# A two-layer transformer kernel: how the position bias rows are repeated 128 times through device memory

## Chip, cores and metric

The kernel runs on one core of a Trainium2 chip, as one program. The metric is the device time of one execution in microseconds (us). The kernel before takes 2340.94 us, the median of 3 runs (2340.61 to 2341.34).

## What is computed

The reference is one block of a first model (four mixers side by side, then a gated feed-forward layer) and two layers of a second model (an attention layer, then a retention layer), on 256 tokens of width 2048 in float32. The change touches the first mixer, an attention with three branches whose scores all get a position bias from a small table:

```python
def rel_bias_heads(dist, table):
    b = table[rel_bucket(dist)].astype(jnp.float32)
    b = jnp.moveaxis(b, -1, 0)
    return b.reshape(NSA_KV_HEADS, NSA_GQA, *dist.shape)
...
    s_w = jnp.einsum('btgrd,bsgd->bgrts', qblk, kw).astype(jnp.float32) * scale + rel_bias_heads(d_w, rel_table)
    p_w = masked_softmax(s_w, m_w)
```

The bias of a head depends only on the distance between query and key. So one row of 512 numbers per head (eight heads) holds all of it, and the score tile of 128 queries needs that row once per query, shifted by one element from each query to the next.

## The kernel before

**The weight stream.** All the weights pass through the core once, in units of at most 128 x 1024 float32 (512 KB). `load` (line 354) issues a unit's load on the SP queue into one of four tiles `wf`; `prefetch` (362) lets ACT round it to its high part `wh` (line 374), and `low` lets DVE make the low part `wl` (line 387), in four tiles each. A `wf` tile is free for the next load when its `wl` is made. PE multiplies with both parts: `job_N` (455) has the tokens stationary and makes three products per step (lines 473, 474, 475), `job_T` (416) has the weights stationary and makes two (lines 449, 450). The jobs run in the order of `plan`.

**The jobs around the change.** After the queries (512 columns) comes the job of the keys `kn` (line 692, 280 columns), then that of the values `vn` (line 693, 256 columns, 16 k tiles x 2 token tiles x 3 products = 96 products, in four units of 512 KB), then the first projection of the fourth mixer, `ev_dqk(0)` (line 923, 16 k tiles x 2 column tiles = 32 pairs of products), then `ev_dqk(1)` (line 929), between whose products those of line 927 stand. The text calls the four units of the value job V0 to V3 and the first of the next job D0.

**The side programs.** `Sched` (274) steps small programs between the products: each `yield n` lets n ticks of 650 ns of planned PE time go by before the next piece is put into the engines' instruction streams. Every engine executes its stream in order. Three side programs matter here:

- `bias_task` (631) makes the bias rows. PE picks the table's rows with a one-hot matrix, DVE copies the 8 x 512 result to SBUF (`rb`, line 641), and POOL issues four DMAs (line 644), each of which writes two of the eight rows 128 times into a tile `dr` in device memory. POOL then issues four loads (line 652) that read `dr` with a shift of one element per partition into the tiles `bias`.
- `zb_task` (680) gives POOL a few operations (`zT`, `zb`) that fall between the first of those DMAs and the other three.
- `task_qk` (877) normalises queries and keys. POOL squares them (`sqq` and `sqk`, lines 882 and 884), DVE reduces them and scales `qn`, and PE transposes the result (`mA`, lines 902 and 908). It begins after the value job, and its first transposes stand in PE's stream after 23 of the 32 pairs of the next job.

Nothing reads `bias` before `task_A` (line 779), long after these jobs. But POOL's stream has the four loads of line 652 ahead of `sqq`, and each of them waits until the DMA of line 644 that wrote its rows has landed.

Of the kernel before, what the change touches and what calls it, by code (L numbers as in the profile page):

```python
# [18 lines left out]
P = 128  # L19
T = 256  # L20
# [14 lines left out]

# ---------------------------------------------------------------- weight plan
def plan():
# [94 lines left out]
def units(jobs):  # L132
    """(stage, offset, words per partition) of every unit, in the order of use"""
    off, out = {}, []
    for j in jobs:
        st = j["stage"]
        nc_ = sum(len(t[1]) for t in j["tiles"])
        K = len(j["rows"])
        sizes = [(min(j["kc"], K - c) * nc_, False) for c in range(0, K, j["kc"])]
        if j.get("raw"):  # L140
            sizes = [z for n in sizes for z in (n, (1024, True))]
        j["u0"] = len(out)
        for n, raw in sizes:
            assert n <= 1024
            o = off.get(st, 0)
            out.append((st, o, n, raw))
            off[st] = o + P * n
    return out, off


# ---------------------------------------------------------------- constants of the shapes
def shape_consts():
# [52 lines left out]
def pack_inputs(inp):  # L205
    """arrays for the device: layout only"""
    f = {k: np.asarray(v) for k, v in inp.items()}
# [64 lines left out]

# ---------------------------------------------------------------- the program
class Sched:
    """side programs, stepped between the matrix products of the weight stream; a program yields the
    number of ticks to wait, or another program whose end it waits for"""

# [45 lines left out]
class XS:  # L323
    """operand tiles [P, hi | lo]; a side program that still has to write one is run on first use"""

# [9 lines left out]
def body(tc, a, out, stop=None, dbg=None):  # L335
# [13 lines left out]

    # ---- weight stream  # L350
    wf, wh, wl = {}, {}, {}
# [10 lines left out]
    def prefetch(to, alt=None):  # L362
        """high parts of the units before to, low parts of those before to - LAG; all in tiles of alt, if given"""
        to = min(len(us), to)
        while pos["sp"] < to:
            load(pos["sp"] + WFB)
            q = pos["sp"]
            st, o, n, raw = us[q]
            if not raw:
                if alt is None:  # L370
                    wh[q] = pw.tile([P, 1024], F32R, name="wh", tag="wh", bufs=4)
                else:
                    wh[q] = alt.tile([P, 1024], F32R, name="wh", tag="wh", bufs=2)
                ACT.activation(wh[q][:, :n], wf[q][:, :n], AF.Copy)  # L374
            pos["sp"] += 1
        low(to if alt else to - LAG, alt)
# [39 lines left out]
    def job_T(j, xs, evac, tail=1, alt=None, raw=None, one=False):  # L416
        """weights stationary: psum [column, (token by x hi) | (token by x lo)] per 128 columns;
        the last units (tail) go column by column; raw: products with the raw units, between the others;
        one: all three products into the same columns"""
        K, nt, kc = len(j["rows"]), len(j["tiles"]), j["kc"]  # L420
# [34 lines left out]
    def job_N(j, xs, evac):  # L455
        """x stationary: psum [token, column] per 128 tokens"""
        K, kc = len(j["rows"]), j["kc"]
# [25 lines left out]

    # ---- small helpers
    def small(w=1, dt=F32):
        return psm.tile([P, w], dt, name="sm", tag=f"sm{w}", bufs=10 if w <= 2 else 4)

    def rsqrt(dst, src, mul, add, w, np_=P):
        """dst = (src * mul + add) ** -0.5; mul None: src ** -0.5"""
        t = small(w)[:np_]  # L490
# [14 lines left out]
    def split(x, src, g=None):  # L505
        """generator: x[:, :T] = hi, x[:, T:] = lo of src * g"""
        if g is None:
# [8 lines left out]
    def put(xs, n, k, src, g=None):  # L516
        """side program: xs[k] = split of src * g"""
        def gen():
# [9 lines left out]
    def col_sums(pp, tag, tiles):  # L528
        """psum [tok, 2n]: column sums of the n tiles [P, T]"""
        pcs = pp.tile([P, 512], F32, name="pcs", tag=tag)  # L530
# [7 lines left out]
    def rms_rows(pp, tag, ss, n, rc, dg, dst):  # L538
        """generator: rc [tok, 2] = rstd columns of the sums ss [P, T]; dst [P, T] = their row broadcast"""
        ps = col_sums(pp, tag, [ss])  # L540
# [8 lines left out]

    # ---- constants  # L550
    NVEC = 7 * 16 + 2 + 12 + 8 + 16
# [15 lines left out]

    # ================================================================ phase 1: mixers
    p12, p1 = ExitStack(), ExitStack()
# [8 lines left out]
    def load_x(order):  # L578
        """x as 8 tiles of two k tiles each"""
        r = []  # L580
# [50 lines left out]
    def bias_task():  # L631
# [9 lines left out]
        V.tensor_copy(rb[:8, :], pb[:8, :])  # L641
        dr = pd.tile([8, P, 512], F32, name="dr")
        for z in range(4):
            G.dma_start(dr[2 * z:2 * z + 2], rb[2 * z:2 * z + 2, None, :].to_broadcast([2, P, 512]))
            yield 7
        d = dr[:]
        for z in range(4):
            yield 2
            bias[z] = s2("bias", (P, 2, T))
            src = bass.AP(tensor=d.tensor, offset=d.offset + 127 + z * 2 * P * 512,  # L650
                          ap=[[511, P], [P * 512, 2], [1, T]])
            G.dma_start(bias[z], src)
# [16 lines left out]

    # ---- A projections  # L670
    zT = s2("zT", (P, 2, T))
# [23 lines left out]
    def gelu2(x, w, mk, e=G):  # L695
        """generator: 2 * gelu(x) (tanh form)"""
        q = mk("gq")[:, :w]
# [11 lines left out]
    def finish_nat(po, kb, tt, mt):  # L709
        """generator: group rms norm of po [tok, 512] and transposition into xB[kb:kb+4]"""  # L710
        jk = s2("jk")
# [32 lines left out]
    def task_A():  # L744
        # compressed keys and values
        hh = yield from gelu2(hx[:, :30], 30, lambda n: small(32), V)
# [32 lines left out]
        yield tBias  # L779
        # attention batches: heads of one kv group per psum bank  # L780
        for tt in range(2):
# [95 lines left out]
    def task_qk():  # L877
        """queries, keys: rms norm per head, transposition; gates"""
        V.tensor_scalar(gq8, gqk[:, 0:1], 0.125, None, OP.mult)
# [33 lines left out]

    # ---- D projections, with the compression products of A behind the first
    dqk = [[s2("dqk", (P, 2, T)) for _ in range(2)] for _ in range(2)]
# [21 lines left out]

    # ---- D: stick breaking
    def task_D():
# [74 lines left out]

    # ---- C: spatial gating
    cv, cu = [None] * 2, [None] * 2
# [35 lines left out]

    # ---- B: gated short convolution
    braw = [s2("braw", (P, 2, T)) for _ in range(2)]
# [70 lines left out]

    # ---- output projection of the mixers
    acc2 = q1.tile([P, T], F32, name="acc2")
# [57 lines left out]

    # ================================================================ phase 2: feed forward
    t1 = s1
# [66 lines left out]

    # layer norm after a residual sum, on shifted values
    class LN:
        tag = "m"

        def __init__(self, pool, x, pair):
            """x: the operand tiles of the residual; pair(k): the tile of the sums k and k + 1"""  # L1260
            self.base = pool
# [9 lines left out]
        def pre(self):  # L1271
            """side program: xr[k] = ALPHA * x[k]"""
            for k in range(16):
# [25 lines left out]
        def add(self, k):  # L1299
            """xr[k] is complete"""  # L1300
            if k < 8:
# [34 lines left out]
        def sums(self, s, q, last):  # L1336
            """column sums"""
            for z, t in ((0, s), (2, q)):
# [4 lines left out]
        def finish(self):  # L1343
            """row broadcasts [P, T]: rstd in psum and in sbuf, -mean * rstd in psum"""
            ps = self.ps
# [32 lines left out]

    # ================================================================ phase 3: attention
    p3l, p3 = ExitStack(), ExitStack()  # L1380
# [39 lines left out]
    def qk_task(key, which, hi, lo, rs, fold):  # L1420
        """rms norm, rope, transposition of 4 heads; rs [P, head, tt]"""
        x = [raw.pop((key, tt)) for tt in range(2)]
# [37 lines left out]
    def og_task(h, o):  # L1460
        """generator: gate and split; o is in psum or sbuf"""
        s = sl.pop(h)
# [114 lines left out]
    def pair0(k):  # L1577
        """in the operand tiles that are read by then"""
        if k in (0, 14):
# [13 lines left out]
    def decay():  # L1593
        """lgd = log1p(-2 ** -e)"""
        ne, fr, u, t, z = [small(16) for _ in range(5)]
# [71 lines left out]

    # ================================================================ phase 4: retention
    qkr, vhl, onT = {}, {}, {}
    spare = [0]  # L1670

    def xa_tile(name, shape=(P, 512)):
        """scratch in the operand tiles that are free until the gates of the first heads"""
        spare[0] += 1
# [212 lines left out]
```

## Time and profile before

| | us |
|---|---|
| median of 3 runs | 2340.94 |
| lowest and highest run | 2340.61, 2341.34 |
| the profiled execution, first to last instruction (span) | 2356.2 |
| PE busy in it | 2285.8 (97%) |
| DVE busy | 1531.2 (65%) |
| ACT busy | 1141.5 (48%) |
| POOL busy | 418.2 (18%) |

Of the profiled execution only the span is known; it is 15.3 us longer than the median of the runs. PE is the engine to look at: it is busy nearly all the time, so the questions are where its few idle stretches lie and what ends them. "DMA share" in the profile is the busy share of the core's 16 DMA engines. The profile counts POOL's queue of DMAs as q0 (software_dynamic) and the queue of the weight loads, which SP issues, as q1 (hardware_dynamic).

### The profile page before, as it was taken

The numbers are of one execution on the slowest core, as the hardware profiler recorded it, in microseconds if no ns is written. First come the engines' busy times: TensorE is split into PE (matmuls) and PEld (weight loads), VectorE is DVE, ScalarE is ACT, GpSimd is POOL, SyncE is SP. The second block draws the span as 40 slices with busy tenths as digits, with TensorE's granted clock in tenths as the row PEclk, the third lists the DMA queues.
The fourth block names the chain that finished last, engine by engine and source line by source line (L and its number), as shares of the span: only waits on it lengthen the run. The fifth ranks groups of instructions, "written<-read, shape, count | busy, mean of one in ns | idle before, by whom it ended". The sixth has DMA issues, their size and how long they took to land.

```text
span 2356.2 us, 33516 instructions
## 1 busy us (share of the span) xinstructions
PE 2285.8 (97%) x12755; PEld 1969.4 (84%) x12755; DVE 1531.2 (65%) x2372; ACT 1141.5 (48%) x1690; POOL 418.2 (18%) x408
## 2 busy tenths in 40 slices
PE   8599999999999999999999999989999999999997
PEld 7487788888888888888888888878888888888887
DVE  6266688765555555555558898867776766777464
ACT  5246654554443344444444556455444544446343
POOL 3114342111110011110002211461000000001061
PEclk9799999999999999999999999989999999999998
DMA  6554346555656555556565444535555555556543
GB/s 217 139 175 142 99 145 212 186 181 188 189 187 188 187 182 190 183 180 193 180 208 181 149 152 153 171 126 194 173 175 179 179 161 180 171 177 192 185 166 119
DMA packets 118641, 408.56 MB, mean 173 GB/s; under 512 B 16490, under 2 KB 18794, under 8 KB 118480
## 3 DMA queue, kind: packets, MB, share of 16 engines
q1 hardware_dynamic: 113184, 400.80, 52.9%
q0 software_dynamic: 5152, 5.54, 1.4%
q8 instruction: 100, 1.64, 0.3%
q14 instruction: 61, 0.50, 0.1%
q10 hardware_dynamic: 144, 0.08, 0.0%
HBM read 402.15 MB, written 4.19 MB: 172 GB/s over the span
## 4 chain that ended last, share of the span: by engine, by line
PE 81%; DVE 6%; POOL 3%; issue 2%; ACT 1%; POOLq 0%; ACTq 0%; DVEq 0%
PE st L449 40%; PE st L450 21%; PE st L473 5%; PE st L474 4%; PE st L475 4%; DVE wl L387 2%; POOL xr L1294 1%; PE mO L1806 1%; PE st L446 1%; PE st L447 1%; PE mA L851 0%; PE mS L1779 0%; POOL lnq L1321 0%; PE mO L832 0%; PE mT L1824 0%
## 5 line engine op out<-in xcount | busy, mean ns | idle before, releaser
L387 DVE TENSOR_TENSOR wl<-wf,wh 128x1024 fp32r<-128x1024 f32 (+1 forms) x750 | 947.9, 1273 | 336.6 <-ACT wh L374 333.0
L374 ACT ACTIVATE wh<-wf 128x1024 fp32r<-128x1024 f32 (+1 forms) x750 | 788.4, 1055 | 730.9 <-PE st L449 439.9
L449 PE MATMUL st<-xA,wh 128*128 128x512 f32 x2144 | 772.1, 403 | 14.9 <-DVE xA L514 7.0
L450 PE MATMUL st<-xA,wl 128*128 128x256 f32 x2272 | 642.3, 283 | 4.2 <-DVE wl L387 4.2
L449 PE MATMUL st<-xB,wh 128*128 128x512 f32 x1536 | 546.3, 399 | 5.8 <-DVE evs L660 2.8
L449 PEld LDWEIGHTS st<-xA,wh 128*128 128x128 f32 x2144 | 406.4, 190 | 115.7 <-ACT wh L374 7.3
L450 PEld LDWEIGHTS st<-xA,wl 128*128 128x128 f32 x2272 | 433.9, 191 | 6.1 <-DVE wl L387 5.9
L450 PE MATMUL st<-xB,wl 128*128 128x256 f32 x1536 | 430.6, 280 | 0.0
L449 PEld LDWEIGHTS st<-xB,wh 128*128 128x128 f32 x1536 | 289.0, 188 | 76.7 <-DVE xB L1652 4.1
L450 PEld LDWEIGHTS st<-xB,wl 128*128 128x128 f32 x1536 | 290.5, 189 | 1.1
L449 PE MATMUL st<-act,wh 128*128 128x512 f32 x704 | 248.8, 399 | 0.0
L450 PE MATMUL st<-act,wl 128*128 128x256 f32 x704 | 197.7, 281 | 0.0
L474 PE MATMUL st<-wl,xB 128*128 128x512 f32 x448 | 174.8, 390 | 0.8 <-DVE wl L387 0.8
L473 PE MATMUL st<-wh,xB 128*128 128x512 f32 x448 | 175.4, 391 | 0.0
L475 PE MATMUL st<-wh,xB 128*128 128x512 f32 x448 | 174.5, 390 | 0.0
L449 PEld LDWEIGHTS st<-act,wh 128*128 128x128 f32 x704 | 132.3, 188 | 33.0
L660 DVE TENSOR_TENSOR evs<-st,evt 128x256 f32<-128x256 f32 x110 | 46.1, 422 | 151.2 <-ACT evt L658 151.2
L450 PEld LDWEIGHTS st<-act,wl 128*128 128x128 f32 x704 | 133.0, 189 | 0.0
L1207 POOL TENSOR_TENSOR evs<-evs,R 128x256 f32<-128x256 f32 x44 | 32.4, 735 | 487.3 <-DVE evs L660 487.3
L1750 POOL TENSOR_TENSOR rm<-qkr,c 128x512 f32<-128x512 f32 x16 | 32.5, 2031 | 456.3 <-DVE qkr L1684 451.7
L474 PEld LDWEIGHTS st<-wl,xB 128*128 128x128 f32 x448 | 84.2, 188 | 17.7 <-DVE wl L387 1.6
L475 PEld LDWEIGHTS st<-wh,xB 128*128 128x128 f32 x448 | 84.1, 188 | 17.7
(425 smaller groups left out, 2621.4 us busy)
## 6 DMA issues: line engine op xcount, KB each, us to landing
wf<-in_w_c SPq DMA_DIRECT2D x264, 512.0 KB, 4.2
wf<-in_w_e SPq DMA_DIRECT2D x256, 512.0 KB, 4.0
wf<-in_w_d SPq DMA_DIRECT2D x112, 512.0 KB, 3.6
wf<-in_w_a SPq DMA_DIRECT2D x84, 512.0 KB, 3.7
wf<-in_w_b SPq DMA_DIRECT2D x32, 512.0 KB, 4.3
xr<-in_xT SPq DMA_DIRECT2D x16, 256.0 KB, 5.9
wf<-in_w_a SPq DMA_DIRECT2D x5, 420.0 KB, 3.9
dr<-rb POOLq DMA_DIRECT2D x4, 512.0 KB, 48.2
```

Of the source, the lines that this page charges most:

```text
L374: ACT.activation(wh[q][:, :n], wf[q][:, :n], AF.Copy)
L387: V.tensor_tensor(wl[q][:, :n], wf[q][:, :n], wh[q][:, :n].bitcast(F32), OP.subtract)
L446: PE.matmul(ps[m][:, :T], hv[:, cs], x[:, :T], start=kk == 0, stop=False)
L447: PE.matmul(ps[m][:, :T], hv[:, cs], x[:, T:], start=False, stop=False)
L449: PE.matmul(ps[m], hv[:, cs], x, start=kk == 0, stop=False)
L450: PE.matmul(ps[m][:, :T], lv[:, cs], x[:, :T], start=False, stop=kk == K - 1)
L473: PE.matmul(p, xh, h[:, o:o + n], start=kk == 0, stop=False)
L474: PE.matmul(p, xh, l[:, o:o + n], start=False, stop=False)
L475: PE.matmul(p, xl, h[:, o:o + n], start=False, stop=kk == K - 1)
L660: V.tensor_tensor(s, p[:, :T], t, OP.add)
L1207: G.tensor_tensor(s, s, R2, OP.mult)
L1750: G.tensor_tensor(m, x[:, ::-1], rsn.rearrange("p (a t) -> p a t", a=2), OP.mult)
```

## The change

The eight rows are first written once, by one DMA, to a tile `d0` of 8 x 512 in device memory (16 KB). A second DMA then reads those 16 KB 128 times (a step of 0 in its source) and writes 128 rows of 16 KB, each with all eight heads. The four loads into `bias` read the new layout: the step from one partition to the next is 8*512 - 1 elements, and that from one head to the next is 512. The rest of the program is the same; other lines of the diff only remove comments.

```diff
@@ -639,16 +639,19 @@
         PE.matmul(pb[:8, :], tb[:33, :], oh[:33, :], start=True, stop=True)
         rb = s2("rb")
         V.tensor_copy(rb[:8, :], pb[:8, :])
-        dr = pd.tile([8, P, 512], F32, name="dr")
-        for z in range(4):
-            G.dma_start(dr[2 * z:2 * z + 2], rb[2 * z:2 * z + 2, None, :].to_broadcast([2, P, 512]))
-            yield 7
+        d0 = pd.tile([8, 512], F32, name="d0")
+        G.dma_start(d0, rb[:8, :])
+        yield 7
+        dr = pd.tile([P, 8 * 512], F32, name="dr")
+        s0 = d0[:]
+        G.dma_start(dr, bass.AP(tensor=s0.tensor, offset=s0.offset, ap=[[0, P], [1, 8 * 512]]))
+        yield 7
         d = dr[:]
         for z in range(4):
             yield 2
             bias[z] = s2("bias", (P, 2, T))
-            src = bass.AP(tensor=d.tensor, offset=d.offset + 127 + z * 2 * P * 512,
-                          ap=[[511, P], [P * 512, 2], [1, T]])
+            src = bass.AP(tensor=d.tensor, offset=d.offset + 127 + z * 2 * 512,
+                          ap=[[8 * 512 - 1, P], [512, 2], [1, T]])
             G.dma_start(bias[z], src)
```

POOL's stream around these DMAs, before (a wait on DMASW is one for a DMA that POOL issued itself):

```order
L644 DMA dr<-rb 256x1x512 [waits DVE_49]
L683 TENSOR_TENSOR zT<-evs,R_121 128x256 [waits Activation_49]
L683 TENSOR_TENSOR zT<-evs,R_121 128x256
L687 TENSOR_TENSOR zb<-zT,v_117 128x480 [waits DMASW2_49,Pool_49]
L687 TENSOR_TENSOR zb<-zT,v_117 128x480 [waits Pool_49]
L644 DMA dr<-rb 256x1x512 x2
L644 DMA dr<-rb 256x1x512 [waits DMASW0_49]
L652 DMA bias<-dr 128x2x256 [waits DMASW5_49,DMASW1_49]
L652 DMA bias<-dr 128x2x256 [waits DMASW6_49]
L652 DMA bias<-dr 128x2x256 [waits DMASW7_49,DMASW3_49]
L652 DMA bias<-dr 128x2x256 [waits DMASW4_49,DMASW0_49]
L882 TENSOR_TENSOR sqq<-qn 128x512 [waits Activation_49]
```

One of the four writes stands ahead of `zT` and `zb` and three behind them, and every `bias` load waits for a write of its own. The same stretch of POOL's stream in the changed kernel, whose line numbers are 3 higher behind the change:

```order
L643 DMA d_479<-rb 8x512 [waits DVE_49]
L686 TENSOR_TENSOR zT<-evs,R_121 128x256 [waits Activation_49]
L686 TENSOR_TENSOR zT<-evs,R_121 128x256
L690 TENSOR_TENSOR zb<-zT,v_117 128x480 [waits DMASW2_49,Pool_49]
L690 TENSOR_TENSOR zb<-zT,v_117 128x480 [waits Pool_49]
L647 DMA dr<-d_479 128x4096 [waits DMASW5_49]
L655 DMA bias<-dr 128x2x256 [waits DMASW6_49]
L655 DMA bias<-dr 128x2x256 [waits DMASW0_49]
L655 DMA bias<-dr 128x2x256 [waits DMASW1_49]
L655 DMA bias<-dr 128x2x256
L885 TENSOR_TENSOR sqq<-qn 128x512 [waits Activation_49]
```

The four writes have become a small one ahead of `zT` and one copy behind `zb`; the copy waits for the small write (DMASW5), and the first `bias` load for the copy (DMASW6). The compute instructions, and their order on every engine, are the same in both kernels.

## Rows read from the trace of the kernel before

**Rows 1.** Windows: us; busy time and instructions of each engine; granted clock; DMA share, GB/s.

```profile
59.40:119.00 59.60, 35.02 (x168) 29.98 (x168) 17.62 (x28) 13.77 (x20) 8.91 (x10) 0.77 0.60 143
119.00:138.00 19.00, 19.00 (x137) 17.64 (x136) 9.80 (x22) 6.66 (x9) 2.12 (x3) 1.00 0.54 187
```

**Rows 2.** Waits of PE between 57 and 119 us: total us, times, longest.

```profile
PE st L473 <- ACT wh L374: 8.7, 3, 6.6
PE st L449 <- ACT wh L374: 6.8, 2, 6.4
PE mA L902 <- DVE qn L894: 4.7, 1, 4.7
```

**Rows 3.** Timeline of ACT, 45 to 130 us: start, us, instruction, idle time before it.

```profile
71.33 1.06 ACT L374 ACTIVATE wh<-wf 128x1024 fp32r<-128x1024 f32 x1 [5.30 <-DMA wf<-in_w_a]
```

**Rows 4.** DMA of 52 to 82 us: queues (packets, MB, share of 16 engines), one issue.

```profile
q0 software_dynamic: 1956, 1.39, 44.8%
q1 hardware_dynamic: 642, 2.37, 21.6%
...
wf<-in_w_a SPq DMA_DIRECT2D x5, 512.0 KB, 26.7
```

**Rows 5.** DMA of 119 to 157 us: the weight loads, KB each, us to landing.

```profile
wf<-in_w_a SPq DMA_DIRECT2D x14, 512.0 KB, 3.9
```

**Rows 6.** Timeline of PE, 52 to 165 us.

```profile
59.16 0.29 PE L475 MATMUL st<-wh,xA 128*128 128x280 f32 x1
...
73.70 0.39 PE L474 MATMUL st<-wl,xA 128*128 128x256 f32 x1 [0.68 <-DVE wl L387]
...
86.06 0.28 PE L475 MATMUL st<-wh,xA 128*128 128x256 f32 x1
...
88.57 0.28 PE L475 MATMUL st<-wh,xA 128*128 128x256 f32 x1
...
104.17 0.39 PE L449 MATMUL st<-xA,wh 128*128 128x512 f32 x1
...
107.64 0.39 PE L449 MATMUL st<-xA,wh 128*128 128x512 f32 x1
...
112.88 1.12 PE L902 MATMUL mA<-ident,qn 128*128 128x128 f32 x4 [4.73 <-DVE qn L894]
...
118.99 0.31 PE L927 MATMUL mB<-zb,wf 128*128 128x30 f32 x2
...
128.70 0.60 PE L902 MATMUL mA<-ident,qn 128*128 128x128 f32 x4
...
129.35 0.31 PE L927 MATMUL mB<-zb,wf 128*128 128x30 f32 x2
```

**Rows 7.** Timeline of POOL, 30 to 180 us.

```profile
43.04 1.09 POOL L644 DMA_DIRECT2D dr<-rb  x1 [12.09 <-DVE rb L641]
...
49.41 3.23 POOL L644 DMA_DIRECT2D dr<-rb  x3
...
106.64 0.71 POOL L652 DMA_DIRECT2D bias<-dr  x1 [3.51 <-DMA dr<-rb]
107.38 1.42 POOL L882 TENSOR_TENSOR sqq<-qn 128x512 f32<-128x512 f32 x1
```

**Rows 8.** DMA before 60 us: the smallest of POOL's loads, KB, us to landing.

```profile
sm<-in_table POOLq DMA_DIRECT2D x1, 1.0 KB, 5.9
```

**Rows 9.** Timeline of SP's queue, 50 to 51.2 us.

```profile
50.38 0.33 SPq L359 DMA_DIRECT2D wf<-in_w_a  x1
```

**Rows 10.** The page, part 3: loads of instructions, packets, MB, share of 16 engines.

```profile
q8 instruction: 100, 1.64, 0.3%
```

**Rows 11.** DMA of 106 to 119 us: POOL's queue, with the bias loads.

```profile
q0 software_dynamic: 118, 0.37, 10.0%
```

**Rows 12.** DMA of 43.5 to 49.4 us, one dr DMA in flight: GB/s in 40 slices.

```profile
GB/s 159 205 410 410 501 342 273 182 76 91 213 233 248 217 157 26 64 4 30 29 29 28 28 28 0 28 28 28 28 28 28 167 83 361 111 139 83 222 361 333
```

## The prediction

> **What bounds the kernel now.** PE is busy for nearly all of the span, so I first looked for the stretch where it is not. The windows show one: from the end of the key job at 59.4 us to the first product of `ev_dqk(1)` at 119.0, PE works 35.0 of 59.6 us, at a mean granted clock of 0.77; in the 19 us behind it, it works all the time at full clock [rows 1, 6]. The waits of PE say what it lacks there: six longer waits, five of them for ACT's `wh` (8.7 + 6.8 us) and one for the scaled `qn` (4.7 us) [rows 2]. ACT in its turn waits for weight loads [rows 3]. So the question is why the loads are late. They take 26.7 us from issue to landing there, and 3.9 us from 119 us on [rows 4, 5]. Yet the queue is not full of bytes: in 30 us q0 moves 1.39 MB and q1 2.37 MB [rows 4]. What differs is the price of a byte. q0 holds 44.8% of 16 engines for 30 us, 215 us of engine time, or 155 us per MB; q1 takes 21.6%, 104 us, or 44 us per MB. A weight load is done only when its last share is, so it waits for the engines on which `dr` writes stand. The wait for `qn` has the same root: POOL cannot begin `sqq` until 107.38, since its last `bias` issue, at 106.64, waited for the last `dr` DMA; PE's transposes follow 5.5 us after `sqq` began [rows 6, 7].
>
> **Most that can be gained.** I rebuild the 59.6 us from full-clock rates. 96 value products at 0.1195 us (21 steps from 86.06 to 88.57) are 11.5 us; 32 pairs at 0.347 us (10 pairs from 104.17 to 107.64) are 11.1 us; the transposes cost 0.65 us (128.70 to 129.35) [rows 6]. Together 23.25 us. If nothing stalled, 59.6 - 23.25 = **36.35 us** would go. 24.6 us of that is idle time, and 11.8 us (35.0 - 23.25) is work at the lower of the two clock levels, 1.2 instead of 2.4 GHz, behind the six waits: 2.0 us for each [rows 1, 2].
>
> **The small write, d0.** It takes the place of the first `dr` DMA, issued at 43.04. The nearest row is the smallest of POOL's loads, which lands 5.9 us after its issue: 48.9 [rows 7, 8]. POOL works on `zT` and `zb` until 49.41 anyway, so I cost this write, and the new wait for it, at nothing. Without that cover it would delay the copy by 5.9 us at most, and no engine but POOL would wait. The three further `dr` issues (3.23 us) become one of about 1.1 us, done at 50.5 [rows 7].
>
> **The copy.** No row before shows a copy inside device memory. It moves 128 x 16 KB = 2.10 MB in 128 rows. I assume that it spreads over all 16 DMA engines as a weight load of 128 rows does. Its engine time is then bounded from below by the price of a weight byte, 44 x 2.10 / 16 = 5.7 us per engine, and from above by the price of a `dr` byte now, 155 x 2.10 / 16 = 20.3 us [rows 4]. The row nearest in kind has the same packet size out of device memory: 100 loads of instructions, 16 KB each, at 0.3% of 16 x 2356 us, 1.13 us each [rows 10]. Eight of those per engine give **9.0 us**, which I take.
>
> Against that choice stands a measurement in the Trainium skill (DMA: Bandwidth & Descriptors, "Latency and other measured facts"): 128 x 16 KB tiles between device-memory tensors went at 207 GB/s per direction where the row pitch was 512 KiB. By my estimate from that page the copy would take 10.1 us and the result would be 2311.1; no run here shows such a copy yet.
>
> **What the copy costs PE.** V0 is issued before 50 us and lands before the copy starts. V1 is issued at 50.38, with the copy [rows 9]. Alone it lands after 3.9 us [rows 5]. If the engines alternate between the two queues, all of the copy goes by while V1's eight packets per engine do: it lands at 54.3 + 9.0 = 63.3. PE has done V0 at 59.4 + 24 x 0.1195 = 62.3, and can go on with V1's second product 2.4 us after ACT has V1 (71.33 to 73.70) [rows 3, 6]: 65.7. PE stalls 3.4 us and loses 2.0 us more to the clock: **5.4 us**. V2, V3 and D0 stand behind V1 in the queue and need 8 x 0.18 us each at a weight byte's price (4 KB at 44 us per MB), faster than the 2.9 us in which PE uses a unit, so they stall nothing. With 5.7 us instead of 9.0 V1 is ready at 62.4 and the cost is nothing; with 20.3 it is 14.7 + 2.0 = 16.7 us.
>
> **The bias loads.** The copy lands at 50.5 + 5.9 + 9.0, plus 4.3 us for three weight units between its packets: 69.7. Four issues of some 0.7 us make POOL free at 72.5, and the transposes could follow 5.5 us later, at 78.0. In PE's stream they come at 59.4 + 11.5 + 5.4 + 23 x 0.347 = 84.3. So the wait of 4.7 us goes, with 6 us to spare; at 20.3 us for the copy both times move and 6 us stay. The loads themselves hold 10.0% of 16 engines x 13 us for 0.37 MB, 56 us per MB [rows 11], so 3.7 us per engine. They fall beside the second unit of `ev_dqk(0)`, which can be issued when V1 is split, near 66 us, and would land at 66 + 3.9 + 3.7 = 73.6; PE wants it at 76.3 + 2.8 = 79.1. I cost them at nothing; this cover is 5 us thick. What stalls next, if anything, is `ev_dqk(1)`, whose eight units come faster than others; it ran without a wait before [rows 1], and the loads ahead of it are less late now.
>
> **Sum.** 36.35 - 5.4 = 31 us less: 2356.2 becomes 2325.2 in a profile. The runs are 15.3 us (0.65%) shorter than the profiled span; on 31 us that is 0.2 us, so I take the difference as it is: 2340.9 - 30.9 = **2310.0 us**. The bounds of the copy give 36.35 - 0 = 2304.6 and 36.35 - 16.7, so 2321.3.
>
> **Rivals.**
>
> *The copy is slower than its bound, but pays.* Between 20.3 and 40 us per engine it eats part of the gain; at 30 us the stall is 24.4 + 2.0 us, 10.0 us are gained, 2331. For it: a fourfold packet does not have to cost four times. Against it: both nearest rows are under 21 us.
>
> *All readers meet at one place: slower.* The copy reads the same 16 KB 128 times. Today's `dr` writes are slow in just this way: one of them alone (out of two partitions) moves about 28 GB/s in the slices in which nothing else runs, and four together only 1.39 MB in 30 us, 46 GB/s [rows 12, 4]. If the bytes of `d0` come at 28 GB/s as well, the copy takes 75 us, on all 16 engines; V1 is ready at 54.3 + 75 + 2.4 = 131.7, PE stalls 69.4 + 2.0 us, and the kernel takes 2376. It decides from the point where the copy takes 40 us (52 GB/s): there stall and clock use up the 36.35 us. Against it: 28 GB/s for one and 46 for four look like a limit of the two or eight partitions that are read, and the copy reads none.
>
> The Trainium skill speaks on both sides here. Its page SBUF — State Buffer ("Door 1: The DMA port swizzle") puts partitions 0 to 3 on one DMA port and 4 to 7 on another of 16 that share 436 GB/s; by my estimate 27 GB/s for one `dr` write and 54 for four, and the trace's 28 and 46 agree. The same page ("A bandwidth-pool intuition that's wrong") gives device memory 32 ports of about 22.5 GB/s: if 16 KB lie on one of these, the copy takes 93 us by my estimate and the kernel is slower by some 50 us. Nothing in this trace shows which.
>
> *Nothing comes of it.* The loads could be late for another reason than `dr`, or the time could come back as waits further on: 2341. Against it: the loads are prompt again as soon as `dr` has landed [rows 1, 5], and PE is the bound behind this stretch.
>
> **How the numbers follow.** Forecast 0.83; slow but paying copy 0.07; nothing 0.04; slower 0.06. Over 0.2% (4.7 us, about what a measurement of this kernel can tell from no change) faster are the first two, 0.90; same 0.04; slower 0.06. The range takes the bounds of the copy with a microsecond for the rest at either end: 2303 to 2322, which leaves the other 0.17 out.
>
> **What would show it.** In the profile after: PE without a wait over 6 us between 59 and 90 us, the first product of line 930 (927 before) near 88 us instead of 119; weight loads of that stretch landing in 4 to 15 us; `sqq` no longer PE's last wait; one `dr` copy that lands within 20 us of its issue. If the loads around the copy land later than 25 us, the price of the copy is wrong; if PE waits for `qn`, the path over POOL is; if the stretch shrinks by 30 us and the time does not, the claim that PE is the bound behind it is.

## The result, and the profile after

| | before | changed |
|---|---|---|
| median, lowest to highest of 5 runs each on one chip, us | 2341.34 (2340.61 to 2355.07) | 2308.87 (2307.98 to 2322.28) |
| span of the profiled execution, us | 2356.2 | 2320.5 |

The changed kernel is faster: the ratio is 0.9848, with a 95% interval of 0.9819 to 0.9877. 2310.0 us were forecast, within 2303 to 2322. The medians differ by 32.5 us, the two profiled executions by 35.7. Some executions of either kernel take about 13 us longer, at another pace of later products, and both profiles shown are of such executions; where the runs of an experiment below lie in two groups, this is why.

Where the time came from is read first in the windows of the changed kernel, whose columns are those of [rows 1]. The second window begins at 59.4 us, where the key job ended before, and ends behind the first product of line 930 (927 before), which stands among those of `ev_dqk(1)`:

```profile
43.00:59.40 16.40, 16.40 (x121) 15.89 (x121) 6.00 (x5) 6.32 (x9) 6.50 (x7) 1.00 0.75 249
59.40:85.00 25.60, 25.09 (x175) 23.17 (x175) 18.59 (x29) 13.27 (x21) 8.63 (x10) 1.00 0.74 256
85.00:104.00 19.00, 19.00 (x133) 17.49 (x132) 10.85 (x24) 7.03 (x11) 1.59 (x2) 1.00 0.63 206
```

PE idles for 0.5 us of 25.6 where it had idled for 24.6 of 59.6, and its granted clock is 1.00 where it had been 0.77. The stretch ends at 82 us instead of 119. The second window has about the PE work of the first one of [rows 1] (175 and 168 records), without the waits. The timeline of PE marks the places that [rows 6] marks:

```profile
57.91 0.28 PE L473 MATMUL st<-wh,xA 128*128 128x256 f32 x1
...
61.59 0.39 PE L474 MATMUL st<-wl,xA 128*128 128x256 f32 x1 [0.51 <-DVE wl L387]
...
78.34 0.60 PE L905 MATMUL mA<-ident,qn 128*128 128x128 f32 x4
...
82.16 0.31 PE L930 MATMUL mB<-zb,wf 128*128 128x30 f32 x2
```

From the end of the key job, where the value job's first product now follows at once (57.91), to the first product of line 930, at 82.16, go 24.25 us; before, from 59.4 to 118.99, 59.6. That is 35.35 us less in this stretch, of 35.7 in the whole profile. The agreement is not exact: the stretch begins 1.5 us earlier than before, nearly all of it ahead of the change's first DMA (issued at 41.66, before at 43.04 [rows 7]), and 1.1 us are lost again behind it. The transposes of `qn`, at 78.34, wait for nothing. ACT has V1 at 58.84 us:

```profile
58.84 1.06 ACT L374 ACTIVATE wh<-wf 128x1024 fp32r<-128x1024 f32 x1 [5.06 <-DMA wf<-in_w_a]
```

All waits of PE from 40 to 125 us in the changed kernel (before, the same answer had the 20 us of [rows 2] at its head):

```profile
PE st L474 <- DVE wl L387: 0.5, 1, 0.5
PE mA L815 <- DVE sm L812: 0.4, 1, 0.4
```

POOL's timeline shows the new small write, the copy, and what waited for each:

```profile
41.66 0.53 POOL L643 DMA_DIRECT2D d<-rb  x1 [11.25 <-DVE rb L641]
...
48.03 0.58 POOL L647 DMA_DIRECT2D dr<-d  x1
...
58.03 2.88 POOL L655 DMA_DIRECT2D bias<-dr  x4 [9.41 <-DMA dr<-d]
60.93 1.49 POOL L885 TENSOR_TENSOR sqq<-qn 128x512 f32<-128x512 f32 x1
```

`sqq` begins at 60.93, where it had begun at 107.38 [rows 7]. The issues of DMAs between 40 and 85 us, with KB and median us to landing:

```profile
wf<-in_w_a SPq DMA_DIRECT2D x14, 512.0 KB, 5.0
dr<-d POOLq DMA_DIRECT2D x1, 2048.0 KB, 9.7
bias<-dr POOLq DMA_DIRECT2D x4, 256.0 KB, 5.9
...
d<-rb POOLq DMA_DIRECT2D x1, 16.0 KB, 2.6
```

And the queues while the copy runs, 49.0 to 57.3 us, with packets, MB and share of 16 engines:

```profile
q0 software_dynamic: 143, 2.10, 71.1%
q1 hardware_dynamic: 139, 0.51, 22.3%
...
wf<-in_w_a SPq DMA_DIRECT2D x4, 512.0 KB, 10.1
```

All 2.10 MB of the copy go by in these 8.3 us. It holds 0.711 x 16 x 8.3 = 94 us of engine time, 45 us per MB or 5.9 us per engine. The old writes held 155 us per MB [rows 4]. The weight loads beside the copy land after 10.1 us, not 26.7. Their own packets were never the dear ones: beside the slow writes a weight byte cost 44 us per MB [rows 4], and from 119 to 157 us in the kernel before, with the writes gone, 0.581 x 16 x 38 / 7.32 = 48:

```profile
q1 hardware_dynamic: 2010, 7.32, 58.1%
```

So the loads were late because their packets waited, not because these were slow.

### The profile page after: what moved, and what is told of

Same layout as the page of the kernel before. It is cut to its first block, busy times and chain, and to the rows that moved or that the text cites. A ratio compares the mean times of both kernels' runs of the same rounds, so it can differ in the third digit from the quotient of the medians.

```text
span 2320.5 us, 33510 instructions
## 1 busy us (share of the span) xinstructions
PE 2276.0 (98%) x12755; PEld 1963.9 (85%) x12755; DVE 1532.2 (66%) x2372; ACT 1141.5 (49%) x1690; POOL 414.8 (18%) x406
## 4 chain that ended last, share of the span: by engine, by line
PE 83%; DVE 5%; POOL 3%; issue 2%; ACT 1%; DMA 0%; POOLq 0%; ACTq 0%; DVEq 0%
PE st L449 41%; PE st L450 22%; PE st L473 5%; PE st L474 4%; PE st L475 4%; DVE wl L387 2%; POOL xr L1297 1%; PE mO L1809 1%; PE st L446 1%; PE st L447 1%; PE mA L854 1%; PE mS L1782 0%; POOL lnq L1324 0%; POOL lny L1649 0%; PE mO L835 0%
## 5 line engine op out<-in xcount | busy, mean ns | idle before, releaser
L1753 POOL TENSOR_TENSOR rm<-qkr,c 128x512 f32<-128x512 f32 x16 | 32.5, 2032 | 456.7 <-DVE qkr L1687 451.7
```

Source lines behind the costliest of these rows:

```text
L1753: G.tensor_tensor(m, x[:, ::-1], rsn.rearrange("p (a t) -> p a t", a=2), OP.mult)
```

## The experiments

**Theory A**, at the start: the old writes were slow because all 2.10 MB were read out of the eight partitions 0 to 7 of `rb`, which sit behind two ports by the map that the prediction names; engines that stood on those slow pieces kept every weight load waiting. **Rival B**: what made them slow was how they were cut, into four DMAs that use few engines each. **Rival Q**: much of the gain is POOL's queue, which no longer holds `sqq` back. Each run stands against the kernel before on the same chip, whose median there was 2342.7 to 2343.9 us.

### The source alone: four narrow copies

Here the eight rows go to `d0` as in the change (lines left out below), and then four DMAs cut as before (two rows each) repeat them from there.

```diff
...
-            G.dma_start(dr[2 * z:2 * z + 2], rb[2 * z:2 * z + 2, None, :].to_broadcast([2, P, 512]))
-            yield 7
+            G.dma_start(dr[2 * z:2 * z + 2], bass.AP(tensor=s0.tensor, offset=s0.offset + z * 1024,
+                                                     ap=[[512, 2], [0, P], [1, 512]]))
+            yield 2
```

> The rows go through d0 in device memory as in the change, but are then repeated by four copies of two rows each, 128 times, as before. Theory A (the old writes were slow because eight SBUF partitions served all of their reads): a copy out of device memory is quick even in four parts, four copies land within 20 us, PE stalls at most 3 us, 2309 to 2314. Theory B (they were slow because each was split over two engines only): the copies still take 35 us or more each, weight loads still land after some 25 us, 2330 to 2345.

Measured: 2316.38 us (2314.03 to 2318.99), ratio 0.9887 (0.9872 to 0.9901). Its queues from 52 to 82 us, and the one long wait of PE up to 125 us:

```profile
q1 hardware_dynamic: 1576, 5.74, 53.9%
q0 software_dynamic: 4026, 2.88, 31.8%
...
wf<-in_w_a SPq DMA_DIRECT2D x9, 512.0 KB, 8.1
dr<-d POOLq DMA_DIRECT2D x2, 512.0 KB, 27.3
```

```profile
PE mA L907 <- DVE qn L899: 8.4, 1, 8.4
```

Cut as before but read from device memory, q0 pays 53 us per MB instead of 155 (the bias loads are among its bytes here), and the weight loads land after 8.1 us. PE has no wait for weights. The source alone therefore brings 27 us. The narrow copies still take over 20 us to land (27.3 for these two), where the wide one took 9.7, so POOL's queue keeps `sqq` back, and PE waits 8.4 us for `qn`. This wait I had not priced, and it put the time above what Theory A expected.

Rival B leans on a rule of the Trainium skill (DMA: Bandwidth & Descriptors, "Rules for kernel authors"): an outermost size below 16 confines a DMA to at most as many engines. No run here counts the engines. These copies keep the outermost size of two, and the weights come in time all the same; what is seen here beside that size is the longer landing, not the late weights.

### Narrow copies, with the bias loads later

One line is added to the kernel above.

```diff
             yield 2
+        yield 45
         d = dr[:]
```

> The four narrow copies out of d0 (as in the first of these runs), with the bias loads 45 ticks (29 us) later in POOL's stream, behind the squares and the scaling of both token tiles. If what the four narrow copies lost against the changed kernel was only the wait of PE for qn (8.4 us) behind POOL's queue: 2307 to 2312, like the changed kernel. Rival (the narrow copies take that time from the weights in any case): 2313 to 2319.

Measured: 2308.67 us (2307.46 to 2320.29), ratio 0.9865 (0.9841 to 0.989), the time of the changed kernel. PE's only wait from 40 to 125 us is now one of 1.0 us at line 760. What the narrow copies lost was the wait for `qn` alone.

### The ports: rows on eight ports, rows on one

In the first of these kernels the source stays in SBUF and the four writes stay as they were; only the rows of `rb` stand on partitions 0, 4, 8 ... 28. In the second they stand on partitions 0 to 3 and 32 to 35. The lines that put them there are left out below: DVE spreads the table's columns, and PE's product and its copy have 32 or 64 rows.

```diff
...
-            G.dma_start(dr[2 * z:2 * z + 2], rb[2 * z:2 * z + 2, None, :].to_broadcast([2, P, 512]))
+            G.dma_start(dr[2 * z:2 * z + 2], rb[8 * z:8 * z + 8:4, None, :].to_broadcast([2, P, 512]))
```

```diff
...
-            G.dma_start(dr[2 * z:2 * z + 2], rb[2 * z:2 * z + 2, None, :].to_broadcast([2, P, 512]))
+            p0 = 32 * (z // 2) + 2 * (z % 2)
+            G.dma_start(dr[2 * z:2 * z + 2], rb[p0:p0 + 2, None, :].to_broadcast([2, P, 512]))
```

> The kernel before, with the eight rows on partitions 0, 4, ..., 28 instead of 0 to 7; the four writes are as before. Theory A with the Trainium skill's port map (SBUF - State Buffer, Door 1: The DMA port swizzle): the eight rows are read through eight ports instead of two, a write lands after 15 to 25 us instead of 40 to 55, and most of the gain is there: 2309 to 2320. Theory B (two engines per write): no change, 2336 to 2346.

> The kernel before, with the eight rows on partitions 0 to 3 and 32 to 35, which by the Trainium skill's port map are all on one DMA port. Theory A (the port limits): the four writes together move 28 GB/s instead of 46, need about 75 us, and the weight loads behind them come later still: 2355 to 2385. Rival (what counts is the partition, or the engines per write): as the kernel before, 2337 to 2347.

Measured, on eight ports: 2314.2 us (2312.71 to 2316.48), ratio 0.9878 (0.9863 to 0.9892). On one: 2378.41 us (2371.74 to 2390.09), ratio 1.015 (1.0109 to 1.019). The queues of the kernel with eight ports, 52 to 82 us:

```profile
q1 hardware_dynamic: 1581, 5.75, 56.0%
q0 software_dynamic: 3139, 2.78, 32.0%
...
wf<-in_w_a SPq DMA_DIRECT2D x10, 512.0 KB, 8.0
```

The same window of the kernel with one port, and its waits of PE from 40 to 125 us:

```profile
q0 software_dynamic: 1795, 0.81, 48.5%
q1 hardware_dynamic: 381, 1.40, 13.3%
...
wf<-in_w_a SPq DMA_DIRECT2D x3, 512.0 KB, 45.0
dr<-rb POOLq DMA_DIRECT2D x1, 512.0 KB, 83.4
```

```profile
PE st L473 <- ACT wh L374: 29.7, 4, 15.7
PE st L449 <- ACT wh L374: 3.3, 1, 3.3
PE st L474 <- DVE wl L387: 2.7, 4, 0.7
```

The bytes, pieces and number of the writes are equal in these two and the kernel before; only the partitions of the source differ. With one port q0 moves 0.81 MB in 30 us, 27 GB/s; before, 1.39 MB, 46 GB/s [rows 4]; with eight, 2.78 MB (the bias loads among them) at 55 us per MB, close to the 53 from device memory. The Trainium skill (SBUF — State Buffer, "Door 1: The DMA port swizzle") puts partitions 32 to 35 on the port of 0 to 3, and the two kernels agree with it: 27 GB/s for four writes out of those eight partitions is about what one write alone had had out of two [rows 12]. With eight ports one wait of 3.1 us for `qn` is left, for the reason seen above.

### POOL's queue alone: the bias loads issued late in the kernel before

```diff
             yield 7
+        yield 55
         d = dr[:]
```

> The kernel before, with the four bias loads some 36 us (55 ticks) later in POOL's stream, behind the squares of the queries. The four slow writes stay. My theory (late weights take most of the 36 us, the POOL queue only the wait of 4.7 us and 2.0 us of lower clock behind it): 2331 to 2338. Rival (POOL's queue, held by the bias loads, is the main cause): under 2325.

Measured: 2345.25 us (2342.17 to 2358.52), ratio 1.002 (1.0002 to 1.0037); the seven lower of its ten runs have a median of 2343.67. No gain, where I had expected one. The waits of PE from 40 to 125 us:

```profile
PE st L473 <- ACT wh L374: 9.0, 2, 6.9
PE st L449 <- ACT wh L374: 6.7, 2, 5.9
PE st L474 <- DVE wl L387: 2.5, 4, 0.9
PE mA L903 <- DVE qn L895: 1.4, 1, 1.4
```

The wait for `qn` falls from 4.7 to 1.4 us, as meant, and the waits for weights stay, so Rival Q falls as the main cause. What that gave was lost again: the loads now run at 143 to 155 us, and between 125 and 200 us PE has a wait of 2.5 us for `sm` (line 810), of 0.4 us in the kernel before. Some 2 us more go between 345 and 405 us. The kernels below with four early writes and with one write over eight ports lose as much there (2 to 3 us), so the late loads are not what costs it; the cause stays open.

### How the writes are cut: one joined write, and an early start

In the first kernel one DMA reads all eight rows from the same eight partitions. In the second the four writes are kept but issued at once, ahead of `zT` and `zb`.

```diff
-        for z in range(4):
-            G.dma_start(dr[2 * z:2 * z + 2], rb[2 * z:2 * z + 2, None, :].to_broadcast([2, P, 512]))
-            yield 7
+        G.dma_start(dr, rb[:8, None, :].to_broadcast([8, P, 512]))
+        yield 14
```

```diff
             G.dma_start(dr[2 * z:2 * z + 2], rb[2 * z:2 * z + 2, None, :].to_broadcast([2, P, 512]))
-            yield 7
+        yield 14
```

> The kernel before with its four writes joined into one: one DMA reads the eight rows from the same eight partitions of rb and writes each 128 times (1024 pieces of 2 KB). It can spread over more engines than a write of two rows could. Theory A (the two ports behind partitions 0 to 7 are the limit): the bytes still come at about 46 GB/s, the write lands 40 to 55 us after its issue, about 9 us earlier than the last of the four because nothing of it waits behind other work of POOL; weight loads still land after 20 us or more; 2333 to 2347 us. Rival B (the spread over the engines is what made it slow): the write lands within 25 us and the kernel takes under 2325 us.

> The kernel before with all four writes of dr issued at once, ahead of POOL's two operations on zT and zb, in place of one ahead and three behind. Bytes, pieces and partitions stay as they were. It tells why one joined write out of the same eight partitions took 2330.8 us and not 2343.9. Theory A (two ports, and the start): the writes read through both ports at 46 GB/s from the start, where before the first one ran alone at 28 GB/s for 6 us; the last of them lands 45 to 52 us after its issue, near 92 us in the span; weight loads between 52 and 82 us still take some 25 us; 2328 to 2337 us. Rival B (the joined write gained by its spread over more engines): four separate writes gain nothing but the early start of three of them, the last lands near 100 us; 2338 to 2346 us.

Measured, joined: 2330.75 us (2329.03 to 2333.21), ratio 0.9937 (0.9914 to 0.996), just under what Theory A expected and well above Rival B. Four early: 2338.36 us (2336.38 to 2351.3), ratio 0.9978 (0.9955 to 1.0001). That is just inside what Rival B gave there (2338 to 2346), and so is the last landing, near 100 us; Theory A had wanted 2328 to 2337 and 92 us. DMA of the joined kernel, 52 to 82 us, and its issue of `dr` in 40 to 110 us:

```profile
q0 software_dynamic: 346, 1.42, 42.3%
q1 hardware_dynamic: 585, 2.13, 21.3%
...
wf<-in_w_a SPq DMA_DIRECT2D x5, 512.0 KB, 25.2
```

```profile
dr<-rb POOLq DMA_DIRECT2D x1, 2048.0 KB, 46.4
```

In these 30 us a single DMA moves what four had moved, 1.42 against 1.39 MB, at 143 against 155 us per MB, and the weight loads are as late as ever [rows 4]. 2.10 MB in 46.4 us are 45 GB/s: two ports, however the DMA is cut. What joining gained is the end. POOL's timelines of the joined kernel and of the one with four early writes:

```profile
42.87 1.09 POOL L643 DMA_DIRECT2D dr<-rb  x1 [11.79 <-DVE rb L641]
...
89.58 2.94 POOL L651 DMA_DIRECT2D bias<-dr  x4 [40.28 <-DMA dr<-rb]
```

```profile
42.23 4.29 POOL L644 DMA_DIRECT2D dr<-rb  x4 [11.31 <-DVE rb L641]
...
87.91 0.79 POOL L652 DMA_DIRECT2D bias<-dr  x1 [37.58 <-DMA dr<-rb]
...
99.18 0.72 POOL L652 DMA_DIRECT2D bias<-dr  x1 [3.28 <-DMA dr<-rb]
```

The last bytes are there near 89.6 us with the joined write, 99.2 with four early ones, and 106.6 before [rows 7]; the times are 13.1, 5.1 and 0 us under that of the kernel before. So the early start is worth 5.1 us (with an interval that reaches zero). For the other 8.0 us the traces show where they arise. In the bulk the four early writes are as fast as the joined one (1.41 MB from 52 to 82 us), and by 88 us they have moved nearly all of their 2.10 MB; but they end one by one from 88 to 99 us with the first bias loads beside them, where the joined one ends at once. For the kernel with four early writes, here are q0 from 42 to 88 us and a wait of PE that the joined kernel lacks:

```profile
q0 software_dynamic: 3367, 2.01, 40.9%
```

```profile
PE st L449 <- ACT wh L374: 5.1, 1, 5.1
```

A spread over more engines, Rival B's reason, would have shown in the bulk, and does not; but why the last tenth of a MB takes 11 us was not taken apart further. From the joined write to the changed kernel another 22 us go, and the next section shows that those are the source. With a source that is not slow the cut delays no weights (the narrow copies above), so start and cut count for PE only while two ports are the limit, or through POOL's queue.

### Eight ports and one write: the gain without the copy

The rows stand on eight ports as above (those lines are left out), and one DMA writes them.

```diff
...
-        for z in range(4):
-            G.dma_start(dr[2 * z:2 * z + 2], rb[2 * z:2 * z + 2, None, :].to_broadcast([2, P, 512]))
-            yield 7
+        G.dma_start(dr, rb[0:32:4, None, :].to_broadcast([8, P, 512]))
+        yield 14
```

> As the kernel before with one write in place of four, but the eight rows lie on partitions 0, 4, 8 ... 28 instead of 0 to 7. No d0, no copy inside device memory. Theory A (ports): the one write reads through eight ports and lands 12 to 25 us after its issue, weight loads of the stretch within 15 us, at most one wait of PE of 2 us or more; 2307 to 2314 us, about as the changed kernel. Rival C (it takes a source in device memory): as the kernel before with one write, 2333 us or more.

Measured: 2311.56 us (2307.59 to 2323.03), ratio 0.9861 (0.9823 to 0.9899). The DMAs of 40 to 110 us, and POOL's queue while the write runs, 43.5 to 61 us, ahead of the bias loads:

```profile
wf<-in_w_a SPq DMA_DIRECT2D x25, 512.0 KB, 4.7
dr<-rb POOLq DMA_DIRECT2D x1, 2048.0 KB, 18.2
```

```profile
q0 software_dynamic: 1040, 2.10, 32.5%
```

The write lands after 18.2 us instead of 46.4, and no wait of PE up to 125 us is over 0.4 us. Its bytes cost 0.325 x 16 x 17.5 / 2.10 = 43 us per MB, where the joined write out of two ports paid 143: the same DMA but for the partitions that it reads. `d0` and a copy inside device memory are not needed for the gain; a source that is not behind two ports is.

### What the copy itself costs

Four kernels ask this: the changed kernel again, beside one that makes the copy twice; one that leaves the repetition out and lets the bias loads read `d0` with the shift the other way, so that its scores get the bias values in another order; and one whose copy is cut into four of 4 KB pieces.

```diff
         G.dma_start(dr, bass.AP(tensor=s0.tensor, offset=s0.offset, ap=[[0, P], [1, 8 * 512]]))
+        dr2 = pd.tile([P, 8 * 512], F32, name="dr2")
+        G.dma_start(dr2, bass.AP(tensor=s0.tensor, offset=s0.offset, ap=[[0, P], [1, 8 * 512]]))
```

```diff
-        dr = pd.tile([P, 8 * 512], F32, name="dr")
-        G.dma_start(dr, bass.AP(tensor=s0.tensor, offset=s0.offset, ap=[[0, P], [1, 8 * 512]]))
-        yield 7
...
-            src = bass.AP(tensor=d.tensor, offset=d.offset + 127 + z * 2 * 512,
-                          ap=[[8 * 512 - 1, P], [512, 2], [1, T]])
+            src = bass.AP(tensor=s0.tensor, offset=s0.offset + z * 2 * 512,
+                          ap=[[1, P], [512, 2], [1, T]])
```

```diff
-        G.dma_start(dr, bass.AP(tensor=s0.tensor, offset=s0.offset, ap=[[0, P], [1, 8 * 512]]))
-        yield 7
+        for z in range(4):
+            G.dma_start(dr[:, 1024 * z:1024 * z + 1024],
+                        bass.AP(tensor=s0.tensor, offset=s0.offset + 1024 * z, ap=[[0, P], [1, 1024]]))
+            yield 2
```

> The changed kernel once more, as the measure for the runs beside it: 2307 to 2312, ratio to the kernel before within 0.982 to 0.988.

> The changed kernel with the 2.10 MB copy issued a second time, into a tile that nobody reads. My theory (a copy costs 5.9 us of every DMA engine, and the weights behind it come that much later; the changed kernel has no slack left, PE already waits 0.5 us): 4 to 9 us slower than the changed kernel, 2313 to 2318. Rival (the queue of weight loads runs far enough ahead to take a second copy as well): 2307 to 2312.

> The changed kernel without its copy: the bias loads read d0 directly, with the shift in the opposite direction (the first mixer's scores get bias values in another order). My theory (the copy costs PE almost nothing, a wait of 0.5 us): 2306 to 2311, no different from the changed kernel's 2309. Rival (the copy still costs through the weights it delays): 2298 to 2304.

> The changed kernel with its copy cut into four: each reads two of the eight rows of d0 (4 KB) 128 times and writes 128 pieces of 4 KB, one to each of 128 rows, so each can use all 16 engines. Source, bytes and number of bytes per engine stay; only the piece is a quarter as long and there are four issues on POOL. Theory A (only the place that is read matters): the copies land within 12 us of their issue, weight loads within 12 us, no wait of PE over 2 us before the first product behind key job and value job; 2307 to 2312 us, as the changed kernel. Rival P (the long 16 KB piece is what made the copy cheap, as I assumed when I priced it by 16 KB packets): pieces of 4 KB cost two to three times as much, the copies land after 20 us or more, PE stalls 3 us or more; 2313 us or more.

Measured: the changed kernel again 2308.74 us (2307.28 to 2321.38), ratio 0.9866 (0.984 to 0.9893). Two copies: 2314.61 us (2314.19 to 2325.65), ratio 0.9891 (0.9868 to 0.9913), 5.9 us more. No copy: 2313.14 us, the median of four runs that lie in two pairs (2306.1 and 2306.9, 2319.4 and 2321.3), ratio 0.9884 (0.9852 to 0.9916); the lower pair stands about 1 us under the lowest runs of the changed kernel (2307.28 and 2307.98) and 2 us under the middle of its seven lower runs (2308.75). Four wide copies: 2308.31 us (2306.91 to 2309.47), ratio 0.9841 (0.9808 to 0.9874). PE's waits with two copies, up to 125 us:

```profile
PE st L473 <- ACT wh L374: 1.8, 1, 1.8
PE st L474 <- DVE wl L387: 1.5, 2, 0.9
```

One copy is hidden nearly whole: leaving it out gains 1 to 2 us, which two runs hardly tell from nothing. A second one uses up the cover: PE stalls 3.3 us for weights, and its granted clock is 0.94 from 59 to 90 us, where it was 1.00. The queue of the kernel with four wide copies, 49 to 60 us:

```profile
q0 software_dynamic: 557, 2.07, 55.1%
...
dr<-d POOLq DMA_DIRECT2D x4, 512.0 KB, 7.8
```

0.551 x 16 x 11 / 2.07 = 47 us per MB with 4 KB pieces, 45 with 16 KB: the length of the piece does not matter between these, and nothing is won by cutting the copy. Among all these kernels none is clearly under the changed one and still computes the bias as it does.

## Why the prediction was right

- **What bounds the kernel, and what can be gained.** "Most that can be gained" was put at 36.35 us: 35.35 went in that stretch. The reading that the waits for weights, the wait for `qn` and the lower clock behind them have one root, the slow bytes of the `dr` writes, is shown from several sides: the same writes with the source moved to eight ports, or to device memory, free the loads; with the source on one port they hold them up more (29.7 us in the first row of PE's waits); moving only the bias loads gains nothing. That the limit is the partitions that are read, which the prediction said against its slower rival, is shown too.
- **The small write.** Costed at nothing, and it is: POOL issues the copy at 48.03, straight behind `zb`, without a wait. It lands after 2.6 us, not 5.9.
- **The copy.** This is the term that was mis-sized. I took 9.0 us per engine from 16 KB loads of instructions; it took 5.9, next to my lower bound of 5.7, the price of a weight byte. The choice of that row, "nearest in kind has the same packet size", was wrong: with 4 KB pieces the price is the same, so packet size was nothing to choose by. The price of a weight byte, measured in the same stretch, was the nearer row.
- **What the copy costs PE.** 5.4 us forecast (3.4 of stall, 2.0 of clock); 0.5 us of stall, and no lower clock. ACT has V1 at 58.84, where V1's load was forecast to land at 63.3. By the sentence on the lower bound ("With 5.7 us instead of 9.0 ... the cost is nothing") this follows from the copy's price. But for half a microsecond it is the error in the stretch: 30.95 us less were forecast, 35.35 measured.
- **The bias loads.** POOL free at 72.5 was forecast, and it is at 60.93; with the 5.5 us behind it the forecast had `qn` ready at 78.0, so both are ahead of the transposes, at 78.34, and the wait for `qn` goes either way; but the 6 us to spare hung on a stall that did not come. How real that path is the narrow copies showed: they left POOL held, and 8.4 us of waiting came back.
- **The sum.** 2310.0 against 2308.87. That it is so close is in part luck. With the copy's cost as measured the same sum gives 4.4 us less, 2305.6. Against that stands its base: 2340.94 us was the median of three runs, and the medians of the kernel before beside the experiments, on four chips, were 1.8 to 2.9 us higher (2342.7 to 2343.9). The two errors partly cancel; corrected for both, the forecast would be 2307.4 to 2308.5. The difference of the medians is 32.5 us here and 34.0 where the changed kernel was run again, against 35.7 in the profiles.
- **The signs.** The copy lands within 20 us (9.7), the weight loads of the stretch within 4 to 15 (10.1 beside the copy, 5.0 over 40 to 85 us), `qn` is no wait of PE's any more; the first product of line 930 came at 82.16, ahead of the 88 forecast, by the cost that the copy did not have and by the earlier start of the stretch (57.91, not 59.4).
- **The rivals.** None of the three came about. "The copy is slower than its bound" wanted over 20 us per engine, and it took 5.9; "Nothing comes of it" wanted 2341 us. "All readers meet at one place" wanted 75 us for the copy; 2.10 MB went by in 8.3 us, 250 GB/s. By the figure of 22.5 GB/s for one port of device memory in the Trainium skill (SBUF — State Buffer, "A bandwidth-pool intuition that's wrong") my estimate was 93 us for 16 KB on one port; the run shows nothing like it, so either the 16 KB do not lie on one such port or that figure does not bound the copy, and no run tells which. The Trainium skill's figure of 207 GB/s (DMA: Bandwidth & Descriptors, "Latency and other measured facts"), given for a row pitch of 512 KiB and copies that other engines issue, is near the rate from issue to landing here, 2.10 MB / 9.7 us = 216 GB/s. Used as engine time, as I did, it was too slow: 10.1 us against 5.9.

## What to carry to other kernels

In this kernel a repeating DMA was priced by where it read, not by its bytes: out of eight SBUF partitions it ran at the speed of their one or two ports (27 and 46 GB/s), and the weight loads, whose own bytes cost no more than elsewhere, came late behind it. Divide a queue's share of engine time by its MB, and where two queues differ threefold, look at the partitions of the dear one; then either spread the rows over ports or repeat them from device memory. Before trusting the gain, ask which in-order queue is held by what comes behind the transfer: here a landing at 27 instead of 10 us cost 8.4 us through POOL, though the bytes were cheap.

## What the hardware showed that was not expected

- Reading the same 16 KB of device memory 128 times costs as much per byte as streaming weights: 45 us of engine time per MB, against 44 for the weight loads [rows 4].
- Spread over eight ports, SBUF as a source is about as good for PE as device memory: 2311.56 us with one write that lands after 18.2 us and costs 43 us of engine time per MB, 2308 to 2309 with the copy that lands after 9.7 and costs 45.
- Four DMAs issued together out of two ports end 10 us after one DMA with the same bytes (99.2 and 89.6 us), though both move 1.4 MB in the 30 us from 52 to 82.
